# A two-block transformer layer: constant loads and block-inversion transfers on other queues and at other points, and new durations in the planner's estimate

## The chip, the cores and the metric

The kernel runs on one core of one Trainium2 chip. The metric is the device time of one execution in microseconds (us). The time before is the median of three runs, 894.01 us (892.88 to 894.18). The profiled execution is one more, with times of its own.

## The reference

Two blocks work on x of 256 tokens by 1,024 features in float32. The first computes a mixer (attention with forget gates, and chunked attention with a relative bias), an attention over 256 memory tokens, and a feed-forward with squared ReLU, each between RMS norms. The second is a hybrid layer, cut here to what matters:

```python
points = np.cumsum(np.array(IN_SPLITS))[:-1].tolist()
(g_qkv, g_z, g_a, g_b, a_q, a_k, a_v,
 i_q, i_k, i_w, gate_a, gate_b) = jnp.split(h @ w_in, points, axis=-1)
qkv = jax.nn.silu(causal_short_conv(g_qkv, conv_w))
...
lhs = a_mat + jnp.eye(C, dtype=f32)
sol = lax.linalg.triangular_solve(lhs, rhs, left_side=True, lower=True, unit_diagonal=True)
...
o_att = dsa_sparse_attention(a_q, a_k, a_v, i_q, i_k, i_w)
merged = jax.nn.sigmoid(gate_a) * o_gdn + jax.nn.sigmoid(gate_b) * o_att
x = x + merged @ w_out
h2 = rms_norm(x, norm_mlp_g)
x = x + jnp.square(jax.nn.relu(h2 @ w_mlp_up)) @ w_mlp_down
```

The triangular solve is that of a gated delta rule over 8 heads; the sparse attention selects 64 keys for each query by a small indexer.

## The kernel before

**Main stream.** TensorE (PE) runs products with weights from the first to the last microsecond. A weight matrix is cut into parts of 512 KB (`Part`, L57). SP loads each part into one of four raw buffers (`_dma`, L282); ScalarE (ACT) casts it to a float32r tile, whi (`split_hi`, L291); VectorE (DVE) subtracts to get the rest, wlo (`split_lo`, L295). Each product is three: hi times hi, hi times lo, lo times hi (`mm3`, L232). `gemm_t` (L357) makes transposed results with 256 moving columns, 24 products for a part; `gemm_n_inter` and `gemm_n_skew` make natural ones with 512 columns.

**Look-ahead.** `pump` (L304) splits parts ahead of the one in use: up to `k.ls`, which is 7 in the feed-forwards and 4 from L1300 on, in the middle of the second block. `split_done` (L299) issues the next weight load at once in program order, when a split has been emitted; on SP the load then waits until its raw buffer's last reader, the subtraction on DVE, is done.

**Side chains.** Norms, attention heads, convolution, delta rule and so on are generators, called side chains, whose steps are put between the products. Each `yield` names what the next step reads, or a number of microseconds. After each group of three or more products `tick` (L260) emits the next step of every chain whose inputs are ready by the planner's estimate. All engines take their instructions in program order, so a step that is emitted too early makes its engine wait.

**Estimate.** `Kern.clock` is PE's estimated time. `mm` (L210) adds a duration for each product, `tr` (L223) for each transpose. `Engine` (L86) adds a fixed part and a rate by elements for ACT, DVE, POOL and DMAs. The lines in question:

```python
        if lhsT.dtype == F32:
            self.clock += max(0.06, n * 4 / 2400)
        else:
            self.clock += max(0.107 if lhsT.dtype == F32R else 0.06, n / 2400)
```

A chain of rank 1 or 2 is also held back while ACT or DVE is estimated to be 8 or 4 us behind PE (`LAG`, L25).

**Constants of the second block.** `consts2` (L1051) is a side chain added at the start of the first feed-forward (L1036). Its first step issues eleven DMAs on SP (L1057 to L1070): 88 columns of w_in in two pieces (w<-w_in), the rotary table, the convolution's weights, biases and gains. Later steps make products and masks of them on ACT, DVE and POOL.

**Inversion of the diagonal blocks.** `chain_diag` (L1380) inverts 64 triangular blocks of 32x32. It writes the whole of U (16 matrices of 128x128) to a DRAM scratch, su, reads the diagonal blocks back with one block for each partition (into T's space), runs a loop of 31 steps with two instructions each on GpSimd (POOL, L1402 to L1406, tile TT), writes the result to scratches scr, and reads them back as tpk. All ten DMAs are issued by ACT (`dma = nc.scalar.dma_start`, L1385). After it `merge` (L1429) joins the blocks with small products (xp, yp), and the delta rule `gdn` (L1665) follows, beside the products of the gates.

Of the kernel before, what the change touches and what calls it, by code (L numbers as in the profile page):

```python
# [24 lines left out]
LAG = (1e9, 8, 4)  # how far ACT or DVE may be behind before a side chain of each rank waits  # L25
# [6 lines left out]
def rows(src, r0, nkt, c0, nc_):  # L32
    """[nkt*128, nc_] block of a 2-D DRAM matrix as [128, nkt, nc_]."""
    n = src.shape[1]
    return bass.AP(tensor=src.tensor, offset=src.offset + r0 * n + c0,
                   ap=[[n, P], [P * n, nkt], [1, nc_]])
# [10 lines left out]
def bc(ap, n):  # L47
    """[128, a] -> [128, a, n] with a zero step."""
    return ap[:, :, None].to_broadcast([P, ap.shape[1], n])


def mid(ap, n):
    """[128, a] -> [128, n, a] with a zero step."""
    return ap[:, None, :].to_broadcast([P, n, ap.shape[1]])


class Part:  # L57
    """half a MB of a weight matrix, as the sum of two float32r tiles."""
# [8 lines left out]
def spans(ap):  # L67
    """the (tile, 128-element block) pairs that an access pattern touches."""
# [17 lines left out]
class Engine:  # L86
    """passes instructions on, and follows when an engine would be done with them."""
# [4 lines left out]
    def __getattr__(self, op):  # L92
        f = getattr(self.eng, op)

        def call(*args, **kw):
# [8 lines left out]
            if "dma" in op:  # L104
                cost = self.fixed + 0.0016 * n * aps[0].shape[0] / P
            elif kw.get("op") == OP.pow:
                cost = 0.3 + 0.165 * n
            elif op == "memset":
                cost = 0.05 + 0.0008 * n
            self.k.note("dma2" if "dma" in op and self.name == "act" else self.name, outs, ins, cost)  # L110
# [12 lines left out]
class Bank:  # L123
    """stands for a free PSUM bank among what a side chain waits for."""
# [6 lines left out]
class Side:  # L131
    """a side chain: its generator, when its next step could start, and the chains it waits for."""
# [8 lines left out]
class Kern:  # L141
    """Emission state: pools, the stream of weights, and the side chains that run beside the products."""

    def __init__(self, ctx, tc):
# [8 lines left out]
        self.units, self.n_dma, self.n_split, self.n_used, self.ls, self.held = [], 0, 0, 0, 6, 0  # L153
        BANK.full = lambda: self.nb >= 7
        self.at = dict(act=0.0, dve=0.0, pool=0.0, dma=0.0, dma2=0.0)
        self.done = {}
        self.clock, self.sides, self.busy, self.nb = 0.0, [], False, 0

    # ---- estimates of when the engines are done, used only for the order in which the side chains are emitted
# [11 lines left out]
    # ---- tiles  # L171
# [14 lines left out]
    def bank(self, shape=(P, 512), name="bank"):  # L186
        """a PSUM bank for the products that run in order; side chains make room for it."""
# [4 lines left out]
    def get(self, shape=(P, 512), name="bank"):  # L192
        """a PSUM bank for a side chain, once one can be spared."""
# [4 lines left out]
    def put(self, n=1):  # L198
        """n banks have had their last read."""
# [9 lines left out]
    # ---- tensor engine  # L209
    def mm(self, out, lhsT, rhs, start=True, stop=True):  # L210
# [5 lines left out]
        if lhsT.dtype == F32:  # L216
            self.clock += max(0.06, n * 4 / 2400)
        else:
            self.clock += max(0.107 if lhsT.dtype == F32R else 0.06, n / 2400)
# [3 lines left out]
    def tr(self, out, in_, n=P):  # L223
        self.nc.tensor.transpose(out, in_, self.ident[:n, :n])  # L224
        self.clock = max(self.clock, self.ready(in_)) + 0.107
        self.wrote(out)
# [5 lines left out]
    def mm3(self, out, st, mv, start, stop):  # L232
        """out += (st.hi + st.lo)^T (mv.hi + mv.lo), without the lo*lo part (below 2^-24)."""
# [4 lines left out]
    # ---- side chains: generators that yield what their next step reads  # L238
# [21 lines left out]
    def tick(self):  # L260
        if self.busy:
            return
# [7 lines left out]
    def finish(self, *which):  # L270
        """runs the given side chains, and those they wait for, to their end, in turns."""
# [9 lines left out]
    # ---- weights  # L281
# [17 lines left out]
    def split_done(self):  # L299
        self.n_split += 1  # L300
        while self.n_dma < min(len(self.units), self.n_split + NRAW):
            self._dma()
# [11 lines left out]
    def drop(self):  # L314
        """a part that was held for a second use is in its last one."""
# [9 lines left out]
class XT:  # L325
    """x^T as an exact sum of two float32r parts: [128, KT, 256]."""
# [20 lines left out]
# ---------------------------------------------------------------- products with weights  # L347
# [9 lines left out]
def gemm_t(k, xt, ncols, evac):  # L357
    """(x @ w)^T, 256 columns at a time: evac(i, psum [128, 2, 256]) returns whether it keeps the bank."""
# [12 lines left out]
def mm_n(k, ps, xt, half, p, kt0, w=512, c0=0):  # L371
    """ps[half] += x[half] @ (part p: 2 tiles of 128 rows from kt0)."""
# [7 lines left out]
def gemm_n_inter(k, xt, evac, width=512, nb=1):  # L380
    """one column block (4 parts), the halves in turns: evac(half, [psum])."""
# [10 lines left out]
def gemm_n_skew(k, xt, nblk, evac, width=512, nb=1, before_b=None, before_4=None):  # L392
    """nblk column blocks, all of half A and then all of half B; evac(half, j, [psum]).
    before_4: called ahead of the first product with the last four tiles of x^T."""
# [20 lines left out]
# ---------------------------------------------------------------- norms  # L415
def rstd_col(k, ss, n_in, name="rs"):
    """(sum over the columns of ss + eps)^-0.5, ss [128, 2] of mean squares."""
# [8 lines left out]
def mean_sq(k, srcs, n):  # L426
    """[128, 2] tile of sum(src^2) / n of two [128, 512] (or narrower) sources."""
# [6 lines left out]
def transposes(k, srcs, n=P):  # L434
    """a side chain's bank of [128, 128] transposes."""
# [7 lines left out]
def chain_xt(k, xt, half, xg, rs, kb0=0):  # L443
    """xt[half] = (xg * rs)^T, [128, 512] column blocks of xg."""
# [13 lines left out]
def chain_norm(k, xt, half, x, g):  # L458
    """xt[half] = (rmsnorm(x) * g)^T, x [128, 1024]."""
# [14 lines left out]
def chain_post(k, half, y, gpost, x_old, x_new, gpre, xt):  # L474
    """x_new = x_old + rmsnorm(y) * gpost (or x_old + y), then xt[half] = (rmsnorm(x_new) * gpre)^T.
    y: two psum banks."""
# [36 lines left out]
# ---------------------------------------------------------------- feed-forward  # L513
# [10 lines left out]
def ffn(k, xt, before_b, evac, last=None):  # L524
    """relu(x w1)^2 w2; evac(half, [2 psum banks]), or last(bank, c0, c1) for columns of half B."""
# [75 lines left out]
# ---------------------------------------------------------------- first block  # L601
# [15 lines left out]
def setup_late(k):  # L617
    """constants that the first products do not need."""
    nc = k.nc
    # tri1[p, 0:128] = (p <= i), tri1[p, 128:256] = 1  # L620
# [6 lines left out]
    # mask[t, s] = 0 where s <= t, NEG elsewhere  # L627
# [14 lines left out]
def lanes(k, head, n, w=2, rank=1):  # L642
    """side chains for n heads, w at a time."""
# [6 lines left out]
def join(sides):  # L650
    """a side chain's wait for others."""
# [4 lines left out]
def attn_transpose(k, p, copy):  # L656
    """the 3 blocks of p, transposed."""
# [16 lines left out]
def block1(k, x, mem, w_in, b_fgt, rel, g_fox_out, g_chk_out, w_out, g_mix_pre, g_mix_post,  # L674
# [3 lines left out]
    # ---- x, its norm  # L678
# [9 lines left out]
    # the gain in all partitions: products with 1  # L688
# [17 lines left out]
    def norm_t(half, j):  # L706
        """columns of the norm and their transposes."""
# [27 lines left out]
    # ---- v and the forget logits of the first attention  # L735
# [6 lines left out]
    def fv_evac(half, j, ps):  # L742
        nc.scalar.copy(fv[:, half, 0:260], ps[0][:, :260])
        nc.scalar.copy(fv[:, half, 260:512], ps[1][:, :252])
        # nx = -(f + b), ax = -|f + b|
# [3 lines left out]
    # mm_n takes a part's two column ranges of 260  # L749
# [9 lines left out]
    def chain_forget():  # L759
        # sel[p, h, :] = 1 for p in (h, 32 + h)  # L760
# [6 lines left out]
        # sp = softplus(-x) = -log sigmoid(x), at columns 0..7 and 32..39  # L767
# [7 lines left out]
        # negative cumulative sums, as hi (rows 0..7) and lo (rows 32..39)  # L775
# [24 lines left out]
    # ---- attention with forget gates, beside the products of the chunked attention  # L800
# [6 lines left out]
    def out_norm(o, sums, col, g):  # L807
        """per half: 1 / sums, rmsnorm over the 512 features, transposes."""
# [30 lines left out]
    def fox():  # L839
# [6 lines left out]
        def scores(i):  # L846
            """of heads 2 i and 2 i + 1, whose products lie in the two halves of the array's rows."""
# [31 lines left out]
    # relative bias: rb[p, h, 0:128] for keys 128 back, rb[p, h, 128:256] for the own 128  # L879
# [52 lines left out]
    # ---- keys and values of the memory  # L932
# [7 lines left out]
    # ---- output product, norms  # L940
# [18 lines left out]
    # ---- attention over the memory, head by head beside the product with w_mq  # L959
# [902 lines left out]
```

## Time and profile before

| what | value |
|---|---|
| median of three runs | 894.01 us |
| lowest, highest | 892.88, 894.18 us |
| profiled execution, span from first to last instruction | 896.4 us |
| PE busy | 880.0 us (98%) |
| DVE busy | 588.4 us (66%) |
| ACT busy | 455.0 us (51%) |
| POOL busy | 92.3 us (10%) |
| HBM read, written | 148.08 MB, 2.62 MB |

The span of the profiled execution lies 2.4 us above the median of the runs. Busy shares are means over the whole span. PE's matmuls are pipelined, so its busy time also covers stretches at a lower clock; the granted clock is shown apart, as a share of full speed. An idle time in square brackets stands ahead of the instruction that it delays, with the one that released it. DMA issues appear as instructions of the issuing engine's queue (SPq, ACTq).

### The profile page before, as it was taken

The page shows a single profiled execution, that of the slowest core. Times are in us where ns is not written, and L with a number is a line of the kernel's source. Part 1 is how long each engine was busy: PE and PEld are TensorE (multiplying, and loading weights), DVE is VectorE, ACT ScalarE, POOL GpSimd, SP SyncE. Part 2 cuts the span into 40 slices and gives each one's busy share as a digit, 9 for nine tenths or more (in the row PEclk, how much of TensorE's full clock was granted, in tenths as well). Part 3 has the DMA queues.
Part 4 walks back from the last instruction along what each step waited for, and adds up shares of the span by engine and source line. Part 5 has one row for each costly group of instructions (what it writes and reads, how often), then busy time and mean ns, then how long its engine had stood idle before and what let it go on. Part 6 is the DMA issues. An engine that isn't in the chain of part 4 may idle for free.

```text
span 896.4 us, 14553 instructions
## 1 busy us (share of the span) xinstructions
PE 880.0 (98%) x5704; PEld 779.1 (87%) x5704; DVE 588.4 (66%) x1028; ACT 455.0 (51%) x779; POOL 92.3 (10%) x150
## 2 busy tenths in 40 slices
PE   8999999999999999999999999989999999999998
PEld 6979998898778999998798899968988789999997
DVE  5676664865777555554779969877578785555541
ACT  6674554553556444443565656353564564444440
POOL 3101010100120000000000118800010000000000
PEclk9999999999999999999999999988999999999999
DMA  8982437473478666654632686474225687666521
GB/s 262 292 247 72 142 120 257 120 255 95 125 215 248 186 190 187 191 181 155 162 121 71 188 212 165 141 165 142 71 71 175 201 231 214 191 187 191 195 84 48
DMA packets 166486, 151.65 MB, mean 169 GB/s; under 512 B 22033, under 2 KB 131217, under 8 KB 166418
## 3 DMA queue, kind: packets, MB, share of 16 engines
q1 hardware_dynamic: 149298, 147.05, 54.9%
q10 hardware_dynamic: 17120, 3.67, 2.0%
q8 instruction: 45, 0.74, 0.3%
q14 instruction: 23, 0.19, 0.1%
HBM read 148.08 MB, written 2.62 MB: 168 GB/s over the span
## 4 chain that ended last, share of the span: by engine, by line
PE 79%; DMA 5%; DVE 5%; POOL 4%; ACT 4%; issue 1%; ACTq 0%; POOLq 0%; DVEq 0%
PE gt L211 27%; PE acc L211 20%; PE gs L211 10%; PE gn L211 9%; POOL TT L96 4%; PE tb L224 3%; PE mo L211 3%; DVE wlo L96 2%; ACT whi L96 1%; PE o L211 1%; DMA raw<-in_w_ff_dram 1%; ACT p L96 1%; DMA su<-U 1%; DMA T<-su 1%; PE ops L211 1%
## 5 line engine op out<-in xcount | busy, mean ns | idle before, releaser
L96 DVE TENSOR_TENSOR wlo<-raw,whi 128x1024 fp32r<-128x1024 f32 (+1 forms) x263 | 314.9, 1224 | 118.2 <-ACT whi L96 116.6
L96 ACT CAST whi<-raw 128x1024 fp32r<-128x1024 f32 (+1 forms) x264 | 267.8, 1047 | 81.2 <-DMA raw<-in_w_ff_dram 31.6
L211 PE MATMUL gt<-xhi,whi 128*128 128x256 f32 x832 | 239.3, 288 | 0.0
L211 PE MATMUL gt<-xlo,whi 128*128 128x256 f32 x832 | 233.9, 281 | 0.0
L211 PE MATMUL gt<-xhi,wlo 128*128 128x256 f32 x832 | 233.5, 281 | 0.0
L211 PEld LDWEIGHTS gt<-xhi,whi 128*128 128x128 f32 x832 | 157.1, 189 | 1.9 <-issue 1.3
L211 PEld LDWEIGHTS gt<-xlo,whi 128*128 128x128 f32 x832 | 157.2, 189 | 0.6
L211 PEld LDWEIGHTS gt<-xhi,wlo 128*128 128x128 f32 x832 | 157.0, 189 | 0.0
L211 PE MATMUL acc<-whi,ul 128*128 128x512 f32 (+1 forms) x288 | 106.3, 369 | 0.0
L211 PE MATMUL acc<-whi,uh 128*128 128x512 f32 (+1 forms) x288 | 106.1, 368 | 0.0
L211 PE MATMUL acc<-wlo,uh 128*128 128x512 f32 (+1 forms) x288 | 106.0, 368 | 0.0
L211 PE MATMUL gs<-whi,xhi 128*128 128x512 f32 (+1 forms) x208 | 80.4, 387 | 0.5 <-ACT xhi L96 0.5
L211 PE MATMUL gs<-wlo,xhi 128*128 128x512 f32 (+1 forms) x208 | 78.7, 378 | 0.3
L211 PE MATMUL gs<-whi,xlo 128*128 128x512 f32 (+1 forms) x208 | 78.7, 378 | 0.0
L211 PE MATMUL gn<-whi,xhi 128*128 128x512 f32 x160 | 68.2, 426 | 0.0
L211 PE MATMUL gn<-wlo,xhi 128*128 128x512 f32 x160 | 64.0, 400 | 0.0
L211 PE MATMUL gn<-whi,xlo 128*128 128x512 f32 x160 | 63.8, 399 | 0.0
L211 PEld LDWEIGHTS acc<-whi,ul 128*128 128x128 f32 x288 | 54.1, 188 | 9.8
L211 PEld LDWEIGHTS acc<-wlo,uh 128*128 128x128 f32 x288 | 54.1, 188 | 9.7
L211 PEld LDWEIGHTS acc<-whi,uh 128*128 128x128 f32 x288 | 54.1, 188 | 9.4
L96 DVE TENSOR_TENSOR r<-r 128x512 f32<-128x512 f32 x32 | 22.1, 690 | 57.4 <-ACT r L96 57.4
L96 POOL TENSOR_SCALAR ms<-ss 128x1 f32<-128x1 f32 x20 | 9.2, 461 | 425.8 <-ACT junk L96 425.7
(364 smaller groups left out, 1144.6 us busy)
## 6 DMA issues: line engine op xcount, KB each, us to landing
raw<-in_w_in_dram SPq DMA_DIRECT2D x84, 512.0 KB, 4.5
raw<-in_w_ff_dram SPq DMA_DIRECT2D x64, 512.0 KB, 4.7
raw<-in_w_mlp_up_dram SPq DMA_DIRECT2D x32, 512.0 KB, 5.5
raw<-in_w_mlp_down_dram SPq DMA_DIRECT2D x32, 512.0 KB, 4.3
raw<-in_w_out_dram SPq DMA_DIRECT2D x16, 512.0 KB, 4.3
raw<-in_w_mk_dram SPq DMA_DIRECT2D x8, 512.0 KB, 5.0
raw<-in_w_mv_dram SPq DMA_DIRECT2D x8, 512.0 KB, 3.9
raw<-in_w_mq_dram SPq DMA_DIRECT2D x8, 512.0 KB, 5.1
```

What stands on the lines that cost most here:

```text
L96: f(*args, **kw)
L211: self.nc.tensor.matmul(out, lhsT, rhs, start=start, stop=stop)
L224: self.nc.tensor.transpose(out, in_, self.ident[:n, :n])
```

## The change

The constants' DMAs start 30 us after the chain's beginning by the estimate, and are spread over seven steps. `chain_diag` issues its DMAs on SP. The scratch su holds only the diagonal blocks, written by eight DMAs of 32 partitions and read in whole rows. The two tpk loads wait 8 and then 4 us by the estimate, where one wait of 5 stood ahead of both. From the point where `k.ls` becomes 4 until the end of `chain_diag` a flag, `lazy`, holds a weight load back in program order until its raw buffer's last split is done by the estimate (`refill`, called by `tick` and `split_done`). The durations of products and of small POOL and accumulating ACT instructions in the estimate are new. The diff also takes comments and docstrings out, and adds an empty line in their places; those lines are left out here.

```diff
@@ class Engine
+            elif self.name == "pool" and n <= 128:
+                cost += 0.2
+            elif "accum_out" in kw and self.name == "act":
+                cost += 0.19
@@ class Kern, __init__
+        self.lazy = False
+        self.round = False
@@ def mm
-        if lhsT.dtype == F32:
-            self.clock += max(0.06, n * 4 / 2400)
+        r = lhsT.dtype == F32R
+        if r and not self.round:
+            self.clock += 0.085
+        self.round = r
+        if r:
+            self.clock += max(0.107, 0.0043 + n * 0.000444)
+        elif lhsT.dtype == F32:
+            self.clock += max(0.214, n * 0.00168) * max(0.25, lhsT.shape[0] / P)
         else:
-            self.clock += max(0.107 if lhsT.dtype == F32R else 0.06, n / 2400)
+            self.clock += max(0.06, n * 0.000444)
@@ def tr
+        self.round = False
@@ def tick
+        self.refill()
@@ def split_done
         self.n_split += 1
+        self.refill()
+
+    def refill(self):
         while self.n_dma < min(len(self.units), self.n_split + NRAW):
+            old = self.units[self.n_dma - NRAW]
+            if self.lazy and self.ready(old.hi, old.lo) > self.clock:
+                break
             self._dma()
@@ def consts2
+    yield 30.0
     raw = k.t4([P, KT, 88], name="w88")
     dma(raw[:, :, 0:16], rows(w_in, 0, KT, C_AB, 16))
+    yield 8.0
     dma(raw[:, :, 16:88], rows(w_in, 0, KT, C_IK, 72))
+    yield 12.0
     k.rt = k.keep([P, 2, 96], "rt")
     dma(k.rt, rope_tab.rearrange("(h p) c -> p h c", p=P))
     k.cw = k.keep([P, 24, 4], "cw")
+    yield 8.0
     dma(k.cw, conv_t)
+    yield 5.0
     k.dtb, k.nal = k.keep([P, 8], "dtb"), k.keep([P, 8], "nal")
     dma(k.dtb, bcast_rows(dt_bias, 8))
     dma(k.nal, bcast_rows(a_log, 8))
+    yield 5.0
     qkg = k.t2([P, 2, P], name="qkg")
     dma(qkg[:, 0], bcast_rows(q_norm_g, P))
     dma(qkg[:, 1], bcast_rows(k_norm_g, P))
+    yield 5.0
     k.gng = k.keep([P, P], "gng")
@@ block2
-    k.ls = 4
+    k.ls, k.lazy = 4, True
@@ def chain_diag
-        dma = nc.scalar.dma_start
-        su = k.dram.tile([16, 8, 16 * P + 16], F32, name="su")
+        dma = nc.sync.dma_start
+        su = k.dram.tile([16, 4, 1024], F32, name="su")
...
         for ch in range(2):
-            dma(at(su, ch * 8 * (P * P + P), [[P, P], [P * P + P, 8], [1, P]]), U[ch])
+            for b in range(4):
+                blk = slice(32 * b, 32 * b + 32)
+                dma(at(su, ch * 32768 + b * 1024, [[32, 32], [4096, 8], [1, 32]]), U[ch][blk, :, blk])
         yield 4.0
         for h in range(2):
-            dma(ub[h * 64:h * 64 + 64], at(su, 0, [[32 * P + 32, 64], [P, 32], [1, 32]]))
+            dma(ub[h * 64:h * 64 + 64], at(su, 0, [[1024, 64], [32, 32], [1, 32]]))
...
-        yield 5.0
         for i in range(2):
+            yield 8.0 - 4.0 * i
             dma(tpk[i], scr[i].rearrange("m q i -> q m i"))
...
+        k.lazy = False
         yield TT + [T]
```

## Rows read from the trace of the kernel before

**Rows 1.** Head of the profile page: span, and busy time of each engine

```profile
span 896.4 us, 14553 instructions
PE 880.0 (98%) x5704; PEld 779.1 (87%) x5704; DVE 588.4 (66%) x1028; ACT 455.0 (51%) x779; POOL 92.3 (10%) x150
```

**Rows 2.** Waits of PE over the span: us in total, times, longest

```profile
PE gb L211 <- DMA grow<-in_g_mix_pre_dram: 3.5, 1, 3.5
PE tb L224 <- DVE r L96: 2.2, 1, 2.2
PE ssp L211 <- ACT sq L96: 1.9, 1, 1.9
PE tb L224 <- DVE vc L96: 1.3, 1, 1.3
PE xp L211 <- DVE Z L96: 0.9, 1, 0.9
PE xp L211 <- DVE vs L96: 0.7, 1, 0.7
PE mo L211 <- ACT xhi L96: 0.7, 1, 0.7
...
```

**Rows 3.** Timeline, 244 to 263 us, SP's queue and ACT: start, us, instruction

```profile
244.73 0.38 SPq L96 DMA_DIRECT2D raw<-in_w_ff_dram  x1
245.16 5.77 SPq L96 DMA_DIRECT2D w<-in_w_in_dram  x2
...
255.32 72.22 SPq L96 DMA_DIRECT2D raw<-in_w_ff_dram  x30
...
262.92 1.05 ACT L96 CAST whi<-raw 128x1024 fp32r<-128x1024 f32 x1 [5.35 <-DMA raw<-in_w_ff_dram]
```

**Rows 4.** Timeline, 530 to 586 us, ACT with its DMA queue, then DVE

```profile
530.01 4.41 ACTq L96 DMA_DIRECT2D T<-su  x2
534.47 0.59 ACT L96 COPY aqT<-tb 128x512 f32<-128x512 f32 x1 [9.29 <-issue]
...
580.26 4.45 ACTq L96 DMA_DIRECT2D scr<-TT  x4
584.81 0.63 ACT L96 ACTIVATE ct<-cy 128x512 f32<-128x512 f32 x1 [8.09 <-POOL rq L96]
...
535.83 2.43 DVE L96 SCALAR_TENSOR_TENSOR cy<-gt,cw,cy 128x255 f32<-128x255 f32 x6 [7.53 <-ACT cy L96]
...
585.47 0.69 DVE L96 SCALAR_TENSOR_TENSOR vc<-ct,cy 128x512 f32<-128x512 f32 x1 [5.40 <-ACT ct L96]
```

**Rows 5.** Windows: length, busy PE PEld DVE ACT POOL, granted clock, DMA share, GB/s

```profile
551.00:556.00 5.00, 5.00 (x32) 5.00 (x31) 5.00 (x9) 1.80 (x3) 4.45 (x8) 0.66 0.70 192
...
599.00:610.00 11.00, 10.26 (x140) 8.38 (x136) 10.71 (x25) 4.63 (x12) 0.00 (x0) 0.53 0.68 192
```

**Rows 6.** Chain that ended last, two pieces; then a DMA issue of the page

```profile
270.76 5.66 PE gt L211 x48
...
282.67 11.07 PE acc L211 x48
...
raw<-in_w_in_dram SPq DMA_DIRECT2D x84, 512.0 KB, 4.5
```

**Rows 7.** Chain that ended last, 520 to 582 us: start, us, piece

```profile
520.83 9.11 DMA su<-U
...
530.73 7.54 DMA T<-su
538.49 1.04 POOL TT L96
...
580.29 1.15 POOL TT L96
```

**Rows 8.** Timeline of POOL, 544 to 548 us

```profile
544.08 0.33 POOL L96 TENSOR_TENSOR TT<-TT,T 128x78 f32<-128x78 f32 x1
544.49 3.08 POOL L96 TENSOR_TENSOR TT<-TT 128x78 f32<-128x78 f32 x1
```

## The prediction

> **What bounds the kernel now.** I read the page's busy table first: PE is busy for 880.0 us of a span of 896.4 us [rows 1], so the whole loss that a better order can win back is small. I read the waits of PE next: what the reader is to see is that, apart from the start (3.5 us for a DMA), five waits hold nearly all of the idle time, 2.2, 1.9, 1.3, 0.9 and 0.7 us [rows 2], each in a place that the diff touches; the longest of those left is 0.7 us. Then I followed each back on the timelines of the engine that was late.
>
> The 2.2 us wait lies at 267 us. SP issued one weight load at 244.73, then the constants of the second block, and the next weight load only at 255.32: 10.6 us without a weight [rows 3]. ACT then stood 5.35 us for that load, DVE behind it, and PE behind DVE.
>
> The 1.9 us wait lies at 547 us. ACT stood idle for 9.29 us up to 534.47, behind its own issue of T<-su, which began at 530.01 and took 4.41 us; DVE stood 7.53 us behind ACT [rows 4]. The 1.3 us wait at 589 us has the same form: ACT stood 8.09 us up to 584.81, the last 4.45 us issuing scr<-TT, and DVE 5.40 us behind it [rows 4]. The releaser named there is a POOL tile: the DMA waits for the end of the POOL loop, and ACT's program is in order.
>
> The clock is the second part of the loss. The windows view shows a granted clock of 0.66 over 551 to 556 us and 0.53 over 599 to 610 us [rows 5], that is part or all of the stretch at 1.2 instead of 2.4 GHz, each behind one of these idle stretches (547 and 597 to 600 us). A stretch at clock c loses its length times (1 - c): 5 x 0.34 = 1.7 us and 11 x 0.47 = 5.2 us.
>
> **The change part by part.** About 0.2% (1.8 us) is what a measurement of this kernel can tell from no change.
>
> A, the constants. Their eleven SP DMAs move some 30 to 75 us into the feed-forward and are spread over seven steps. The 10.6 us gap in the weights goes; I take the whole 2.2 us of rows 2. Ends: 0 (the same gap appears later) and 2.2. I take the upper one, because each step now holds SP for at most the two w<-w_in issues, 5.77 us for both [rows 3], now apart, while the feed-forward keeps up to 7 split parts ahead and PE takes 2.83 us for one (48 products in 5.66 us are two parts) [rows 6]: 20 us of cover. If that cover is gone, the part costs what it does now. POOL's masks and the DVE products of the constants move with it, into a stretch where nothing waits for them.
>
> B and C, the inversion's DMAs. Ten DMAs leave ACT's queue and sixteen (eight su, two T, four scr, two tpk) enter SP's. On ACT they stopped the casts, of which only 4 parts were ahead (11.3 us). On SP they stop the weight loads, with four raw buffers ahead of those parts as well: 8 parts, 22.6 us, less the way back of a load, 4.5 us to land [rows 6] and then its two splitting steps. So a hold of SP of up to some 15 us is hidden. B is the write and read of su: the wait of 1.9 us and the 1.7 us of clock go, 3.6 us. C is scr and tpk: 1.3 us goes; the waits of 0.9 and 0.7 us name DVE's Z and vs, which are late because DVE lost 5.40 us to ACT [rows 4], and with them would go the 5.2 us of clock. Of these 6.8 us I take half, 3.4 us, since DVE is busy for 10.71 of 11 us there [rows 5] and may stay late. C is 4.7 us (ends 0 and 8.1).
>
> The su path itself: now 9.11 us for the write and 7.54 us for the read [rows 7]. The new write is 256 KB in 2,048 runs of 128 bytes, a quarter of the bytes of the old one, which had 2,048 runs of 512. Ends: 2.3 us (by bytes) and 9.1 us (by runs); nearest is the old read with 4,096 runs of 128 bytes in 7.54 us, so 3.8 us. Ahead of it stand eight issues on SP; the four of scr<-TT took 4.45 us together [rows 4], and with 256 runs each instead of 1,024 or 2,048 I take 0.5 us for one (ends 0.1 and 1.1). The new read has 128 runs of 4 KB; I take the 4.5 us that a weight load of the same size needs [rows 6]. Some 12 us instead of 17.7, with SP held for 8 of them: the POOL loop starts about 5 us sooner. PE waits for none of this today, so it enters the sum with nothing; it is room for the loop.
>
> The rule that speaks against it is in the Trainium skill, "DMA: Bandwidth & Descriptors", Specifications: below 512 bytes a transfer is a read-modify-write and misses line rate. By that rule the new write would be no faster than the old, 9.1 us and not 3.8; SP would be held for 13 us, close to its cover of 15, and were B's 3.6 us lost to that, the time would be 891.1 us by the rule and 887.5 by the rows. No row here shows a write of 128-byte runs.
>
> The tpk loads are placed 8 and then 4 us apart in the estimate instead of 5 for both: up to 7 us later on that chain, about what the su path gives back.
>
> D, the estimate. The POOL loop is 62 instructions and runs from 538.49 to 580.29, 41.8 us [rows 7]; by the old formula it is 23.8 us, by the new one 34.6. Scr's DMAs and what follows are so placed some 11 us later, and the estimate falls short of the loop by 7 us instead of 18. For PE the old formula says 0.107 and 0.213 us for products of 256 and 512 columns, the new one 0.118 and 0.232; the rows give 5.66/48 = 0.118 and 11.07/48 = 0.231 us [rows 6]. So the new clock is the true one. But the old error of 8 to 10% was a margin: a step that the others need 2 us for was placed 0.17 us late in PE's true time, everywhere in the program. What that margin hid, no row shows. Ends: a gain of some 3 us (the five smaller waits of PE, 0.7 us at most each [rows 2]) and a loss of 0.17 us on some 100 visits of a side chain to PE (24 heads with three each, 4 memory heads with five, and others), 17 us. I take 4 us of loss: PE's remaining waits are few, so most visits have more slack than 0.17 us, but every chain is ordered anew. The lazy refill orders only SP against SP, and costs nothing but an idle raw buffer.
>
> Sum: 2.2 + 3.6 + 4.7 = 10.5 us of gain, less 4: 6.5 us. The profiled execution has a span of 896.4 us, 2.4 above the median of 894.01, so 889.9 in its terms and **887.5 us** as a median.
>
> **The rivals.**
>
> 1. The margin decides (slower). PE is in order: a visit that comes before its operand stops everything. Place: the attention heads of both blocks, where PE now hardly waits [rows 2]. Its price is 17 us at full size; less the gain of 10.5 that is 6.5 us slower, 900.5 us. It decides from a mean of 0.105 us a visit on. Against it: steps are placed only after three or more products (0.35 us and up), which is a margin of its own.
>
> 2. SP's queue takes the place of ACT's. The scr DMAs wait on SP for the POOL loop, which is still 7 us longer than estimated, and then issue for 4.45 us: a hold of some 12 us, with the weights behind it. For it speaks part A's own row: a hold of 10.6 us cost 2.2 us of PE [rows 2, 3]. Then C stays as it is, and the time is 894.0 - 5.8 + 4 = 892.2 us. The POOL loop could grow as well: one instruction of it took 3.08 us where the one before it took 0.33 [rows 8], while DVE ran two 128x1024 subtractions, so a fuller DVE lengthens it. The Trainium skill, "SBUF — State Buffer", Who interferes with whom, says that a DVE instruction with two SBUF inputs and a GpSimd one that reads SBUF lock each other out; the row agrees, and by that rule DVE's regained time adds to the hold and makes this rival the likelier.
>
> 3. DVE is the bound there. It is busy for 5.00 of 5 and 10.71 of 11 us in the slow-clock stretches [rows 5]; freeing ACT then moves no PE wait, and only A is left, less part of D: about 893 us. Against it: DVE's 7.53 and 5.40 us of idle time lie directly ahead of these stretches [rows 4].
>
> **How the numbers follow.** The forecast has 0.54, the margin 0.22, SP's queue 0.14, DVE's bound 0.10. Half of the second rival and a little of the third are faster than 0.2%, a little of both is slower: faster 0.62, within 0.2% 0.13, slower 0.25. The range: all of A, B and C without D's loss is 13.9 us, 880.1; upward it takes in rivals 2 and 3 and the milder half of the margin. 880 to 898 leaves out some 0.2.
>
> **What would show it.** Right: no PE wait of over 1 us near 260 to 270; w<-w_in on SP between 270 and 320; no idle stretch of ACT behind T<-su or scr<-TT; su to T in some 12 us; clock 1.00 where it is 0.66 and 0.53 now. Wrong: PE waits on DVE or ACT in the attention stretches adding up to over 10 us (rival 1); ACT waiting for weight loads and PE behind it 10 to 20 us after the end of the POOL loop, at half clock (rival 2); the same two waits with ACT free and DVE full (rival 3).

## The result, and the profile after

The changed kernel takes **901.94 us** (median of 7 runs, 899.61 to 904.35); the kernel before took 894.88 us beside it (7 runs, 892.88 to 899.34). The ratio is 1.0075, 95% interval 1.0054 to 1.0096: 7 us slower, where 6.5 us faster was forecast. The time lies on the side of the first rival, and above the range. Ratios and intervals here and below leave out one execution in a slow state, the longest of f1 (917.38 us at a mean granted clock of 0.979).

The head of the page, of the execution that was profiled (900.7 us):

```profile
span 898.4 us, 14580 instructions
PE 878.6 (98%) x5704; PEld 776.1 (86%) x5704; DVE 590.6 (66%) x1028; ACT 455.5 (51%) x779; POOL 89.7 (10%) x150
```

The work of every engine is that of [rows 1]. PE stands idle for 898.4 - 878.6 = 19.8 us of the span, against 896.4 - 880.0 = 16.4 us before. These two spans lie only 2.0 us apart where the medians lie 7.1 apart, since the profiled execution of the kernel before was one of its longer ones (mean granted clock 0.992, where after has 0.998). PE has more idle time although its clock was better, so the waits of PE are the next view (us in total, times, longest):

```profile
PE tb L236 <- DVE xg L96: 4.2, 3, 1.7
PE tb L236 <- DVE y L96: 2.6, 2, 2.0
PE gb L217 <- DMA grow<-in_g_mix_pre_dram: 2.3, 1, 2.3
PE s L217 <- DVE ncum L96: 1.6, 1, 1.6
PE ao L217 <- ACT pt L96: 1.4, 2, 1.1
```

The five waits of [rows 2] that the change was to remove are gone: of the tiles that they name only r still has one, of 0.2 us, further down in this view. In their place stand waits that the kernel before had hardly or not at all: the transposes of the norms (xg and y, 6.8 us together), the forget gate's scores (ncum) and one product of the second block's attention (pt). All but the last and one of xg fall before 450 us, in the first block, where the change moves no transfer of this chain and reorders it by the estimate alone.

The moves did what was forecast. SP's queue in the timeline (start, us, what it issued):

```profile
283.27 0.43 SPq L96 DMA_DIRECT2D w<-in_w_in_dram  x1
...
294.69 0.43 SPq L96 DMA_DIRECT2D w<-in_w_in_dram  x1
...
522.77 3.91 SPq L96 DMA_DIRECT2D su<-U  x8
...
528.04 1.19 SPq L96 DMA_DIRECT2D T<-su  x2
...
581.45 4.58 SPq L96 DMA_DIRECT2D scr<-TT  x4
```

The constants' loads take 0.43 us each where two together held SP for 5.77 us [rows 3]. The POOL loop begins 12.7 us after the first su issue, as the timeline of POOL shows (first and last instruction of the loop; before, 17.7 us from the write of su to the loop, [rows 7]):

```profile
535.45 1.27 POOL L96 TENSOR_TENSOR TT<-TT,T 128x31 f32<-128x31 f32 x1 [0.33 <-DMA T<-su]
...
575.37 1.15 POOL L96 COPY TT<-TT 128x512 f32<-128x512 f32 x1
```

The loop ends at 576.52 and scr is issued only at 581.45, behind it: SP isn't held for the loop here. With the old durations it is, as e3 and e4 below show.

What the new waits look like, in the timeline of DVE and PE around the longest y wait:

```profile
84.29 0.69 DVE L96 TENSOR_TENSOR y<-y,gfc 128x512 f32<-128x512 f32 x1 [1.18 <-ACT junk L96]
...
84.90 0.49 DVE L96 TENSOR_SCALAR y<-y,rs 128x512 f32<-128x512 f32 x1
...
85.54 0.63 PE L236 MATMUL tb<-ident,y 128*128 128x128 f32 x4 [1.98 <-DVE y L96]
```

The transposes of the first half of y stand in PE's order ahead of their operand. That operand, y times rs, stands in DVE's order behind the second half's y times gain, which overwrites y and so had to wait 1.18 us for ACT to have read it (junk is the tile into which ACT writes the squares of y, for their sum). And the stop has a second price, in the windows (length, busy PE PEld DVE ACT POOL, granted clock, DMA share, GB/s):

```profile
82.00:84.00 2.00, 1.56 (x14) 1.36 (x12) 1.01 (x3) 0.76 (x3) 0.94 (x2) 1.00 0.19 56
84.00:86.00 2.00, 0.46 (x5) 0.49 (x5) 1.39 (x3) 1.68 (x4) 1.56 (x2) 1.00 0.00 0
86.00:88.00 2.00, 2.00 (x12) 2.00 (x11) 2.00 (x4) 1.53 (x2) 0.07 (x1) 0.52 0.00 1
88.00:90.00 2.00, 2.00 (x13) 2.00 (x12) 1.07 (x1) 0.00 (x0) 0.00 (x0) 0.62 0.92 270
```

PE is idle for 2 us, and then has about half its clock for 4 us: 2 x 0.48 + 2 x 0.38 = 1.7 us more.

### The profile page after: what moved, and what is told of

Its sections match the earlier page's. It is cut to its first block, busy times and chain, and to the rows that moved or that the text cites. A ratio compares the mean times of both kernels' runs of the same rounds, so it can differ in the third digit from the quotient of the medians.

```text
span 898.4 us, 14580 instructions
## 1 busy us (share of the span) xinstructions
PE 878.6 (98%) x5704; PEld 776.1 (86%) x5704; DVE 590.6 (66%) x1028; ACT 455.5 (51%) x779; POOL 89.7 (10%) x150
## 3 DMA queue, kind: packets, MB, share of 16 engines
q10 hardware_dynamic: 576, 1.05, 0.4%
## 4 chain that ended last, share of the span: by engine, by line
PE 76%; DVE 12%; ACT 6%; DMA 4%; issue 2%; SPq 0%; POOL 0%; DVEq 0%; ACTq 0%; POOLq 0%
PE gt L217 22%; PE acc L217 20%; PE gn L217 11%; PE gs L217 10%; DVE wlo L96 5%; PE tb L236 3%; PE mo L217 2%; ACT whi L96 2%; DMA raw<-in_w_in_dram 2%; DVE cy L96 2%; ACT junk L96 1%; PE s L217 1%; PE o L217 1%; PE ops L217 1%; ACT p L96 1%
## 5 line engine op out<-in xcount | busy, mean ns | idle before, releaser
L96 DVE TENSOR_TENSOR wlo<-raw,whi 128x1024 fp32r<-128x1024 f32 (+1 forms) x263 | 314.6, 1224 | 106.9 <-ACT whi L96 105.9
L96 ACT CAST whi<-raw 128x1024 fp32r<-128x1024 f32 (+1 forms) x264 | 267.7, 1047 | 68.3 <-DMA raw<-in_w_in_dram 18.4
L217 PE MATMUL gn<-whi,xhi 128*128 128x512 f32 x160 | 66.4, 415 | 0.0
L96 DVE TENSOR_TENSOR r<-r 128x512 f32<-128x512 f32 x32 | 22.2, 693 | 57.7 <-ACT r L96 57.7
L96 POOL TENSOR_SCALAR ms<-ss 128x1 f32<-128x1 f32 x20 | 10.5, 524 | 441.9 <-ACT junk L96 441.8
```

The costliest lines, as they stand in the source:

```text
L96: f(*args, **kw)
L217: self.nc.tensor.matmul(out, lhsT, rhs, start=start, stop=stop)
```

## The experiments

Theory M is the first rival: the old durations of PE were a margin, the new ones take it away. Theory R was formed on the results of the first eight runs: the order that stood is a favourable one for these durations, and any other order loses, in whatever direction the durations are moved. Other letters are explained in the expectation that names them first. Sixteen kernels were run in four groups; the kernel before had medians of 895.28 (e), 894.52 (f), 895.54 (g) and 894.42 us (h) beside them.

**Which part.** Each part alone, and both moves without the durations.

e1, the kernel before with the new durations and nothing else:

```
+            elif self.name == "pool" and n <= 128:
+                cost += 0.2
+            elif "accum_out" in kw and self.name == "act":
+                cost += 0.19
...
+            self.clock += max(0.107, 0.0043 + n * 0.000444)
```

> The kernel before with the new durations in the planner's estimate alone; the constants, the inversion's DMAs and the order of SP stay. Theory M (the margin): these durations are the loss, since side chains now reach PE before the norms' chains are done; 6 to 14 us slower than before (901 to 909), with PE waits on DVE at tb<-xg and tb<-y that add up to over 5 us. Rival S (SP's queue): the loss comes from the moved DMAs; this kernel is within 3 us of before (892 to 898).

Measured: 907.57 us, ratio 1.0142 (1.0121 to 1.0162), 12.3 us slower. Its waits of PE:

```profile
PE gs L216 <- DVE xlo L96: 3.2, 1, 3.2
PE tb L235 <- ACT p L96: 3.1, 1, 3.1
PE tb L235 <- DVE y L96: 2.6, 2, 2.0
PE tb L235 <- DVE xg L96: 2.5, 3, 1.7
```

The y wait of after is here to the tenth, and xg has the same longest wait, 1.7 us, without any move: the estimate alone makes them.

e2, the kernel before with the constants moved and nothing else:

```
+    yield 30.0
     raw = k.t4([P, KT, 88], name="w88")
...
+    yield 12.0
     k.rt = k.keep([P, 2, 96], "rt")
```

> The kernel before with the constants' DMAs moved 30 us into the feed-forward and spread, alone. Both theories: the PE wait of 2.2 us near 267 us goes and nothing takes its place, 1 to 3 us faster (892 to 894). If the new place only moves the gap in the weight loads, no change within 1 us.

Measured: 890.86 us, ratio 0.9956 (0.9937 to 0.9974), 4.4 us faster, more than the 1 to 3 us expected. The wait for r is gone; those for sq and vc stay:

```profile
PE tb L224 <- DVE vc L96: 1.5, 1, 1.5
PE ssp L211 <- ACT sq L96: 1.4, 1, 1.4
```

e3, the kernel before with the inversion's transfers on SP, the smaller su, the new waits ahead of tpk and the lazy refill:

```
-        dma = nc.scalar.dma_start
+        dma = nc.sync.dma_start
...
+            for b in range(4):
+                blk = slice(32 * b, 32 * b + 32)
+                dma(at(su, ch * 32768 + b * 1024, [[32, 32], [4096, 8], [1, 32]]), U[ch][blk, :, blk])
```

> The kernel before with the inversion's DMAs on SP, the compact scratch, the two waits of 8 and 4 us and the lazy refill, with the old durations. Theory M: the waits of ACT behind its own DMAs go and with them the PE waits of 1.9 and 1.3 us, 2 to 6 us faster (889 to 893). Rival S: SP holds the weight loads for 10 to 20 us behind the POOL loop, 3 to 8 us slower (898 to 903), with PE waits in the 30 us after the loop's end.

Measured: 890.96 us, ratio 0.9952 (0.9934 to 0.9971), 4.3 us faster. Now the wait for sq is gone, with Z and vs, and r stays; vc, which part C was to remove, is longer and goes only in e4:

```profile
PE tb L225 <- DVE r L96: 2.7, 1, 2.7
PE tb L225 <- DVE vc L96: 2.1, 1, 2.1
```

What holds vc up is the second rival's mechanism. SP's queue waits for the end of the POOL loop, and then ACT for a weight (waits of SP: us in total, times, longest; then the timeline of ACT):

```profile
SPq L96 <- POOL TT L96: 14.2, 2, 12.6
```

```profile
586.48 1.05 ACT L96 CAST whi<-raw 128x1024 fp32r<-128x1024 f32 x1 [9.77 <-DMA raw<-in_w_in_dram]
```

From 563.73 to 581.12 us, 17.4 us, SP issues no weight. ACT's part of vc stands in its program behind that cast, and PE waits 2.1 us.

e4, both moves with the old durations (the edits of e2 and e3 together):

> The kernel before with both moves (constants, inversion) and the old durations: the changed kernel without its new durations. Theory M: the gains of the two moves add, 4 to 8 us faster than before (887 to 891), so 11 to 14 us faster than the changed kernel. Rival S: 1 to 6 us slower than before (896 to 901), at most 3 us from the changed kernel.

Measured: **886.80 us** (885.63 to 887.9), ratio 0.9903 (0.9884 to 0.9921), 8.5 us faster, just past the 4 to 8 expected; 4.4 + 4.3 = 8.7, so the two add up. This version beats both kernels. Its page and its waits of PE:

```profile
span 883.9 us, 14576 instructions
...
PE 874.0 (99%) x5704; PEld 775.2 (88%) x5704; DVE 589.8 (67%) x1028; ACT 455.0 (51%) x779; POOL 91.4 (10%) x150
```

```profile
PE gb L212 <- DMA grow<-in_g_mix_pre_dram: 2.3, 1, 2.3
PE tb L225 <- DVE xg L96: 1.3, 1, 1.3
PE tb L225 <- ACT p L96: 0.8, 4, 0.3
PE mo L212 <- ACT xhi L96: 0.7, 1, 0.7
```

PE stands idle for 883.9 - 874.0 = 9.9 us, half of what it does in after, and behind the start only one wait is longer than 0.7 us. Of the 14.5 us between the spans of e4 and after, 9.9 us are idle time; in the other 4.6 us PE counts as busy, of which the mean clock of 0.998 explains some 1.8 us, and the rest is open. The second stretch of [rows 5] is at full clock, with DVE about as full as before (a window; the granted clock is 1.00 over the whole of 530 to 620 us, so also where the same work now stands some 5 us earlier):

```profile
599.00:610.00 11.00, 11.00 (x203) 9.01 (x199) 10.56 (x27) 5.97 (x14) 0.00 (x0) 1.00 0.57 177
```

SP is held here too, from the end of its last weight issue at 559.54 until the next at 574.41, 14.9 us:

```profile
523.10 36.44 SPq L96 DMA_DIRECT2D raw<-in_w_in_dram  x13
570.56 3.76 SPq L96 DMA_DIRECT2D scr<-TT  x4
```

ACT then stands 7.73 us for a weight, and PE waits for nothing: the prediction's cover of some 15 us holds at 14.9 us and not at e3's 17.4.

So the moves are worth 8.5 us, and the new durations on top of them cost 901.94 - 886.80 = 15.1 us. Everything that follows is about these 15.1 us.

**Which durations, and which mechanism.** f1 is both moves with the new durations of PE's products alone; f2 is both moves with the additions for POOL and ACT alone (the two halves of the edit of e1).

> Both moves, and of the new durations those of PE's products alone (rate, switch, small products); POOL's and ACT's additions are left out. Theory M (the old, too fast clock was a margin): the loss is here, 899 to 908, since the clock moves on and the other engines' durations stay as short as they were; PE waits on DVE at tb<-xg and tb<-y as in the changed kernel, or longer. Rival E (the additions for small POOL and accumulating ACT instructions reorder the chains for the worse): within 3 us of the moves alone, 885 to 890.

> Both moves, and of the new durations those for small POOL and accumulating ACT instructions alone; PE's products keep the old ones. Theory M: 884 to 890, near the moves alone, since the additions only place steps later. Rival E: 898 to 904, near the changed kernel.

Measured: f1 902.1 us, ratio 1.0083 (1.0047 to 1.0118), from four executions between 898.7 and 906.5 us; f2 903.87 us, ratio 1.0104 (1.0078 to 1.0131). Each half alone costs what both together do, which no sum over visits can give. By theory M f2 should have been no slower than e4: its additions put steps later and PE's durations are the old ones. The timeline of PE in f2 shows where later is too late:

```profile
678.18 0.40 PE L216 MATMUL gs<-whi,xlo 128*128 128x512 f32 x1
687.66 1.09 PE L229 MATMUL tb<-ident,Z 128*128 128x128 f32 x4 [9.08 <-DVE Z L96]
```

The delta rule's chain was still running when the program forced its end (`k.finish` emits all of its steps at once), and PE stood for 9.08 us; in the next 6 us its granted clock is 0.60:

```profile
688.00:694.00 6.00, 5.85 (x21) 4.54 (x20) 4.58 (x7) 4.55 (x6) 0.00 (x0) 0.60 0.03 6
```

f3 is the kernel after with the margin given back: 1.0 us added to the time from which a step that waits for a tile may be emitted.

```
-        s.at = self.ready(*(r if isinstance(r, (list, tuple)) else [r]))
+        s.at = self.ready(*(r if isinstance(r, (list, tuple)) else [r])) + 1.0
```

> The changed kernel with 1.0 us added to the point from which a chain's next step may be emitted (its inputs' estimated end plus 1.0 us). Theory M: the waits of PE on the norms' chains go and most of the loss with them, 886 to 893. Rival L (with the faster clock ACT and DVE count as less late, chains of rank 1 and 2 are let through sooner and push the splits back on DVE): the margin does not touch this, 898 to 903.

Measured: 901.58 us, ratio 1.0078 (1.0055 to 1.0100): nothing. The waits of its trace moved instead of going; y and ncum fall, Z comes:

```profile
PE tb L236 <- DVE xg L96: 4.0, 3, 1.7
PE tb L236 <- DVE Z L96: 3.1, 2, 2.1
```

f4 is the kernel after with the limits on how far ACT and DVE may be behind halved, LAG = (1e9, 4, 2):

> The changed kernel with the limits on how far ACT or DVE may be behind halved, from 8 and 4 us to 4 and 2 us. Theory M: no gain of over 4 us, 898 to 904, the same waits of PE at tb<-xg and tb<-y. Rival L: most of the loss comes back, 887 to 894.

Measured: 896.09 us, ratio 1.0009 (0.9992 to 1.0025), 5.9 us faster than after, with the y wait still there (`PE tb L236 <- DVE y L96: 3.0, 2, 1.9`). That lies between the two forecasts and decides for neither.

**Where.** g1 is both moves with the new durations up to the start of the second block; g2 has them from there on.

```
+        if not self.meas:
             if lhsT.dtype == F32:
                 self.clock += max(0.06, n * 4 / 2400)
...
 def block2(k, x3, ht, st, out, conv_w, norm_mlp_g):
+    k.meas = True
```

> Both moves, with the new durations up to the start of the second block's products and the old ones from there. Theory T (two sides: in the first block steps now reach PE before the norms' chains are done; in the second a chain that is placed later ends late): 893 to 897, since PE's waits and slow clock of the changed kernel before 240 us, some 8 us more than in the moves alone, stay. Rival L2 (the loss is in the second block, where DVE is full): 886 to 889.

> Both moves, with the old durations up to the start of the second block's products and the new ones from there. Theory T: 889 to 894, the smaller half of the loss, with PE's waits between 440 and 620 us. Rival L2: 897 to 902, all of it.

Measured: g1 896.32 us, ratio 1.0013 (0.9995 to 1.0030), 9.5 us above e4; g2 890.11 us, ratio 0.9960 (0.9929 to 0.9990), 3.3 us above e4. The two make 12.8 of the 15.1 us, three quarters of that in the first block, as theory T forecast; the next four runs contradict T. The trace of g1 has the waits of after:

```profile
PE tb L246 <- DVE y L96: 2.6, 2, 2.0
PE tb L246 <- DVE xg L96: 2.2, 3, 1.4
PE s L218 <- DVE ncum L96: 1.5, 1, 1.5
```

**Which direction.** Both moves, and the old durations of PE times 0.97 (away from the measured ones), 1.05, 0.99 and 1.01:

```
-            self.clock += max(0.107 if lhsT.dtype == F32R else 0.06, n / 2400)
+            self.clock += 1.01 * max(0.107 if lhsT.dtype == F32R else 0.06, n / 2400)
```

> Both moves, PE's old durations times 0.97: a small change away from the measured ones. Theory T (a clock that runs late is a margin in the first block): PE's waits before 240 us stay under 2 us; the time is 885 to 892. Rival R (any new order loses, since the constants beside it were fitted to the old one; the direction does not matter): 893 to 902, about as far from the moves alone as the new durations.

> Both moves, PE's old durations times 1.05: half way to the measured rate, nothing else. Theory T: half of the loss in the first block, 889 to 895, with PE waits on DVE at tb<-y or tb<-xg of 2 to 5 us in all before 240 us. Rival R: 893 to 902, with waits in other places than those of the changed kernel.

> Both moves; PE's old durations times 0.99, which says nothing new of the chip and reorders a little. If the loss comes from PE's durations having gone the wrong way or lost a margin, a change of 1% moves the time by under 3 us from 886.8: 885 to 889. If the order that stood is a lucky one, it loses at random as the 0.97 and the 1.05 did: 892 to 900.

> Both moves; PE's old durations times 1.01. By the lost margin: a tenth of the way to the measured ones, 1.5 us of the 15: 887 to 889 us. By the lucky order: 892 to 900, as far off as 0.99 is, with no order between the two.

Measured: 0.97 gives 899.1 us (ratio 1.0048, 1.0029 to 1.0067), 0.99 gives 898.07 (1.0034, 1.0012 to 1.0055), 1.01 gives 894.71 (0.999, 0.997 to 1.0011), 1.05 gives 897.22 (1.0030, 1.0007 to 1.0054); 1.00 is e4, 886.80 (0.9903). **One per cent either way, which tells the estimate nothing, costs 8 to 11 us**, as much as 3 or 5%. That is as theory R forecast: the times follow no direction along the scale, and the unchanged one is lowest. In h2 and h3 other waits than those of after have come up, here of h3, then of h2:

```profile
PE ao L212 <- ACT pt L96: 3.4, 2, 2.9
PE gs L212 <- DVE xlo L96: 2.3, 1, 2.3
```

```profile
PE tb L225 <- DVE Z L96: 3.0, 2, 2.0
PE gs L212 <- DVE xlo L96: 2.9, 1, 2.9
```

**Is it a wait that the estimate lacks?** The timeline at 84 us showed one: an instruction that overwrites y waits for ACT's reading of it, and the estimate looks at inputs alone. h1 is the kernel after, h4 is e4, each with the estimate also keeping, for every block, the end of the reads by all engines but PE:

```
+        end = max([self.at[eng], self.ready(*ins), self.clock if dma else 0.0]
+                  + [self.used.get(b, 0.0) for a in outs for b in spans(a)]) + cost
...
+        for a in ins:
+            for b in spans(a):
+                self.used[b] = max(self.used.get(b, 0.0), end + 0.15)
```

> Both moves and the new durations, and the estimate also lets an instruction that overwrites a block wait for the end of that block's earlier reads (before, it looked at inputs alone). If the new durations lose because they lay bare a kind of wait that the estimate doesn't know, the waits of PE in the first 270 us fall from 7.9 us to under 3 and the time to 890 or less. If any order other than the one that stood loses 10 us or so, it comes out between 894 and 905 us.

> Both moves and the old durations (886.8 us so far), with that same wait for earlier reads in the estimate. If the wait is a real one that the estimate lacked, 884 to 888 us. If the order that stood is merely the best of many near ones, 890 us or more, though the estimate knows more.

Measured: h1 899.71 us (ratio 1.0058, 1.0036 to 1.0081), h4 895.46 us (0.9997, 0.9975 to 1.0019). In h1 the y wait is gone; xg (3.5 us) and ncum (1.5 us) stay, and two others have come or grown:

```profile
PE tb L241 <- ACT xm L96: 2.8, 1, 2.8
PE tb L241 <- DVE vc L96: 1.7, 1, 1.7
```

Whether y went because the estimate now knows of it, or because the order is another one, h1 can't tell.

h4 knows strictly more than e4 and is 8.7 us slower. Its two worst waits are new as well:

```profile
PE gn L217 <- DVE QE L96: 4.0, 1, 4.0
PE gs L217 <- DVE xlo L96: 2.8, 1, 2.8
```

In all there are thirteen kernels with both moves and an order other than that of e4 (after, f1 to f4, g1 to g4, h1 to h4). They lie between 890.1 and 903.9 us, with a mean of 898.2; e4 at 886.8 lies below all of them. Five of the thirteen carry none of the new durations (g3, g4, h2, h3, h4): 894.7 to 899.1 us, with a mean of 896.9. So of the 15.1 us that the new durations cost, 10.1 us is what leaving the order of e4 costs on the mean, and 5.0 us is left. After, f1, f2 and f3 (901.6 to 903.9) lie above all five, so a part of these 5 us may belong to the new durations themselves. The y wait speaks for it: 2.6 to 3.0 us in after, e1, f1, f4 and g1, which all have PE's new durations in the first block, and at most 0.5 us in every other kernel. How much of the 5 us it makes was not shown.

The sequences of PE's 5,704 products in the traces show how much was reordered. Some 240 products in h2 and 410 in h3 stand outside the sequence that they share with e4, 920 in g2 and 1,420 in after: the loss doesn't go with the number, since g2 loses least. And e4's own order is new, with some 180 products moved against the kernel before, and gains: not every reordering loses.

## Why the prediction was wrong

**A, the constants: right in kind, half its size.** The wait of [rows 2] for r went with the gap in SP's queue, alone (e2) and with the rest (e4). The term said 2.2 us; e2 measured 4.4. What the other 2.2 us are is open: the term has no clock behind this wait, and the profile of the kernel before shows 1.00 from 265 to 285 us, but e3's, where r waits for 2.7 us, has 0.67 from 270 to 275, some 1.6 us. The cover held: no load of a constant stops PE in after.

**B and C, the inversion: right in kind, twice too large.** 3.6 + 4.7 = 8.3 us were forecast, e3 measured 4.3. The waits for sq, Z and vs went with e3, that for vc only with e4, and the granted clock of e4 is 1.00 where [rows 5] has 0.66 and 0.53, as the forecast said. One part of what is missing in e3 is the wait for vc, 2.1 us, which SP's queue now causes. The clock terms, 1.7 and half of 5.2 us, were read from one execution with long half-clock stretches: its span of 896.4 us is a time of some 898.5 (a run's time is 2.3 us over its span in after, 1.9 in e4), and the kernel's typical time is 4 us below that. The errors of A and of B and C nearly cancel, by luck: 10.5 us forecast for the three, 8.5 measured. The sentence that five waits hold nearly all of the idle time was a misreading as well: they make 7.0 us of the 16.4 - 3.5 = 12.9 us behind the start.

**The su path** was forecast at 12 us and is 12.7; eight issues on SP at 0.5 us each, and they take 3.91 us. The rule of the Trainium skill that spoke against it ("DMA: Bandwidth & Descriptors", Specifications: under 512 bytes a read-modify-write) does not set the time here. The DMA issues, for the stretch from 515 to 605 us of after (the last column is the median from issue to landing), and a window while su is written (DMA share and GB/s are its last columns):

```profile
T<-su SPq DMA_DIRECT2D x2, 256.0 KB, 6.3
...
su<-U SPq DMA_DIRECT2D x8, 32.0 KB, 1.7
```

```profile
523.00:526.00 3.00, 3.00 (x21) 2.66 (x20) 2.93 (x8) 2.64 (x11) 0.00 (x0) 1.00 0.38 57
```

So the write in 128-byte runs is over some 3.91 + 1.7 = 5.6 us after its first issue, where the prediction read the rule as the old 9.11 us [rows 7]. It ran beside little other traffic, the old one beside the weight loads. 57 GB/s at a share of 0.38 are 150 GB/s at full share, where the same view of the kernel before has 262 GB/s at 0.98 from 520 to 523 us, with 512-byte runs and weights: a lower rate, as the rule says, but with a quarter of the bytes to write. And writes of short runs did stand in the old trace: two of the four scr<-TT DMAs write runs of 128 bytes and two runs of 64, and they landed in 3.9 us (median). The read was taken at 4.5 us and needs 6.3.

**The second rival (SP's queue) has its mechanism in the runs, but not its price.** With the old durations SP does wait for the loop, 12.6 us in e3 and 11.0 in e4, and issues scr behind it. PE loses 2.1 us to that in e3 and nothing in e4, and both gain. In after scr stands behind the loop, SP is held for its 4.58 us alone, and the rival has no part in the loss. The POOL loop did not grow either: 576.52 - 535.45 = 41.1 us with DVE busy for 99% of it, where it took 581.44 - 538.49 = 43.0 us before [rows 7], with DVE at 95%. **The third (DVE) falls** by e4: DVE is busy for 10.56 of 11 us from 599 on, and PE loses nothing.

**D, the estimate, is the step that failed.** The prediction put it thus: "the old error of 8 to 10% was a margin", ends 3 us of gain and 17 of loss, and "I take 4 us of loss". It measured 15.1 us (12.3 without the moves): inside the ends, near the wrong one. The reason given for 4, that "most visits have more slack than 0.17 us", was an argument about single visits, where "every chain is ordered anew", said in the same sentence, was the term that decided: a reordering that tells the estimate nothing costs 8 to 11 us by itself (h2, h3), and 4 us was too little for it.

The first rival had the sign and nearly the time (900.5), but only a part of the mechanism. Right is that PE's order stops for operands that are not there, and that this appears as waits on DVE and ACT. What the runs show against the margin as the cause is that a loss of this size comes without any loss of margin: f2 leaves PE's durations as they were and loses 17.1 us; g3 and h2 make the old error larger, not smaller, and lose 12.3 and 11.3. f3 gives 1 us back to every step that waits for a tile and gains nothing, which is weaker evidence, since it reorders as well. That the margin has a part in the 5 us left is not excluded. Since most of the loss is the price of another order, it is luck that the rival's 17 us came near the measured 15.1. Nor are the attention heads the main place: in after they have 3.0 us (ncum, pt), the norms 6.8; in other orders it is the delta rule (Z), the split of x^T (xlo) or an attention head (pt in h3).

What the runs show in its place: e4 has 9.9 us of idle PE left in 884 us; each of the thirteen reorderings of it, from whatever cause, puts a few visits ahead of their operands, or a chain behind the point where the program must have it, at up to 9 us a piece and some clock behind the longer ones. If the constants beside the old durations (the waits of 4, 5 and 8 us, the ranks, LAG) had been fitted to them, that would explain why e4 is the lowest of fourteen; it was not shown, since no set of constants was fitted anew to the new durations. f4, where LAG gives back 5.9 us, doesn't decide it: its 896.1 us is also where any other draw would lie. Open, too, is why 10 us is the usual price, and not 5 or 20.

## What to carry to other kernels

Where an order comes out of an estimate, and the constants around the estimate have been fitted on the chip, a more accurate estimate can act as a new draw among orders, as here: price it by what the scatter of orders is, not by the accuracy gained. That scatter can be had before the edit is judged, with two or three runs in which a duration is changed by 1%. And a change that mixes moves of transfers with a new estimate should be measured in its parts: here a gain of 8.5 us lay hidden under 15.1 us of loss.

## What the runs showed of the hardware beyond that

The kernel before scatters by 8.5 us over 31 executions beside the last group, 891.72 to 900.21, and the granted clock of an execution goes with it: 0.998 in the shortest, 0.990 to 0.991 in the three longest. 0.8% of 892 us is 7 us, so by these means most of this kernel's scatter goes with the time that PE spends at its lower clock. e4, whose profile shows no stretch at the lower clock, has a clock of 0.999 or 1.00 in all six runs and a scatter of 2.3 us.

This doesn't carry over to every kernel: g4 scatters by 5.2 us over ten runs at 0.998 to 1.00, and h2, with two waits of 2 to 3 us, by only 3.0 us at 0.994 to 0.996. What stays is the caution: a price for the clock that is read from a single profile can be several us off the median, as the clock terms of B and C were.
